# Three PSUM banks for the attention scores, with the rotated transpositions sharing two banks

## The chip, the core and the metric

One core of one Trainium2 chip runs the kernel. The metric is the device time of one launch in microseconds (us), the median of several runs. PE is TensorE's matmul, PEld its weight load, DVE VectorE, ACT ScalarE, POOL GpSimd, SP SyncE. PSUM is where PE writes its results; the kernel hands it out in eight banks, each of 512 float32 values on 128 partitions.

## The reference

The reference is a two-layer encoder trunk over 1024 tokens of width 1024, in float32. Layer 0 mixes tokens with windowed attention, layer 1 with a gated linear recurrence; each also has 4 cross-attention heads into 256 memory tokens, and ends with a convolutional feed-forward layer. The change is in layer 0's mixer:

```python
def mixer_window_attn(u, mem_kv, w_in, sink, w_out, pos):
    q, k, v, xq = jnp.split(u @ w_in, [ATT_Q_W, ATT_Q_W + ATT_KV_W, ATT_Q_W + 2 * ATT_KV_W], axis=-1)
    q = rope(q.reshape(bsz, t, 16, 64), pos)
    k = rope(k.reshape(bsz, t, 4, 64), pos)
    o = window_gqa_sink(q, k, v, sink).reshape(bsz, t, ATT_Q_W)
    return jnp.concatenate([o, memory_cross_attn(xq, mem_kv)], axis=-1) @ w_out
```

In `window_gqa_sink`, 16 query heads share 4 key heads, four to one. The tokens form 8 blocks of 128. A block's queries see the keys of their own block and of the two beside it, less those further than 128 tokens away, and the softmax has one more term per head, the sink.

## The kernel before

All products are made in float32 parts: an operand is split into a high part, rounded by an ACT cast, and the rest, which DVE subtracts; two or three matmuls take the place of one.

The function `window` computes layer 0's mixer. The source says what is to be done and in which buffer; a planner then orders the instructions of each engine with its own estimates of durations. An instruction that stands earlier in the source has the higher priority, and one of lower priority goes in where PE would otherwise have nothing ready. Each engine then runs its queue strictly in that fixed order. A tile has a tag, and a tag has a number of buffers (`bufs`); a new tile of a tag waits until one of them is free, and a buffer is free when the last reader of its tile is done.

The work runs over four groups `g`, each with four query heads and one key head.

- `proj(g)` projects a group. Its `token(t)` is called for the eight token tiles: 24 matmuls into a bank `pj`, then DVE multiplies by cosine and sine, POOL adds the two into the rotated row `rq` (five buffers), and the values go to `v`.
- `turn(b, rqs)` transposes four of these rows, for half `b` of the tokens. It makes three tiles: `w` 0 and 1 are two query heads each, `w` 2 the keys. Each tile takes four transpositions on PE (line 310), one for each row, and is emptied by an ACT cast and a DVE subtraction for the keys (`split`, lines 85 and 86), or by two of each for the queries (lines 318 to 321). These tiles have a bank of their own, tag `ptq`, except for the queries of group 0's first half, which use the two banks `pt`.
- `attend(g)` goes through the eight blocks. A block has four scores (one per head), each two matmuls (lines 362 and 363) into a bank `ps`; DVE adds the mask, takes the row maximum and writes the score to `sm` (line 365), and with that frees the bank. ACT then makes the exponentials (line 372), ACT and DVE divide, and for each of three key blocks PE transposes the four heads' probabilities into a bank `pt` (line 388), which `split` empties; two matmuls (lines 391, 392) add the product with `v` into the bank `po`. `sm` has three buffers.
- `cross_unit` does half of one cross-attention head. Eight of these are spread behind the blocks, and they use the same tags `pj`, `ps`, `pt` (line 232) and `po`.

The source order is `proj(0)`, then `attend(g)` and `proj(g + 1)` for `g` = 0, 1, 2, then `attend(3)`; so in the planned order the projection of the next group lies in the gaps of this group's attention.

The PSUM banks in this stage are two `pj`, one `ptq`, two `ps`, two `pt` and one `po`, eight together.

Under `attend(3)`, where there is nothing left to project, the output projection fills the gaps. `wo0.begin` computes its first partial sums from heads 0 to 11, eight token tiles one after another; `bank()` gives them the banks of its list in turn (`pj`, `pj`, `ptq`). `wo0.finish` adds a second part: the four cross heads (`cross`) and then heads 12 to 15 (`kept`), which `attend(3)` has just made and `split_moved` (line 341) splits. Its first six token tiles use the same list; from the seventh on it has further banks, allocated where the attention's were.

Of the kernel before, what the change touches and what calls it, by code (L numbers as in the profile page):

```python
# [8 lines left out]
F32 = mybir.dt.float32  # L9
# [9 lines left out]
P = 128  # L19
T = 1024  # L20
D = 1024
NT = T // P
# [24 lines left out]
def build(tc, A, out):  # L47
# [20 lines left out]
    def wunit(src, n=1024, pl=None, eng=None, tags=None):  # L68

        tg = tags or (("wh", "wl") if pl is None else ("xwh", "xwl"))  # L70
        h = (pl or ring).tile([P, 1024], F32R, tag=tg[0], name=tg[0])
        l = (pl or ring).tile([P, 1024], F32R, tag=tg[1], name=tg[1])
        raw = stg.tile([P, 1024], F32, tag="st", name="st")[:, :n]
        nc.sync.dma_start(raw, src)
        act.copy(h[:, :n], raw)  # L75
        (eng or dve).tensor_tensor(l[:, :n], raw, h[:, :n].bitcast(F32), op=ALU.subtract)  # L76
        return h, l

    def mm3(o, ah, al, bh, bl, first, last):
        pe.matmul(o, ah, bh, start=first, stop=False)  # L80
        pe.matmul(o, ah, bl, start=False, stop=False)  # L81
        return pe.matmul(o, al, bh, start=False, stop=last)  # L82

    def split(h, l, src):
        act.copy(h, src)  # L85
        dve.tensor_tensor(l, src, h.bitcast(F32), op=ALU.subtract)  # L86
# [155 lines left out]
    def window():  # L242
        ea = tc.alloc_tile_pool(name="attn0", bufs=1, reuse_waits="tile")
        ap_ = tc.alloc_tile_pool(name="attn", bufs=2, side="right", reuse_waits="tile")
        psq = tc.alloc_tile_pool(name="aps0", bufs=1, space=PSUM, reuse_waits="tile")
        psp = tc.alloc_tile_pool(name="aps", bufs=1, space=PSUM, side="right", reuse_waits="tile")
# [5 lines left out]
        nc.sync.dma_start(sk, A["a_sink"].to_broadcast([P, 16]))  # L252
        c4 = lambda ap: ap.rearrange("p (h a c) -> p h a c", a=2, c=32)

        tags = {"pj": ("pj", 2, psq), "ps": ("ps", 2, psp), "pt": ("pt", 2, psp), "po": [lambda: psp.tile([P, 512], F32, tag="po", bufs=1, name="po")] * 2, "sm": 3}
        xhead = [None]
        def pair(kind, i):
            pl, n = (ea, 1) if kind == "x" else (ap_, 2)
# [4 lines left out]
        def proj(g):  # L263
            us = [wunit(A["wqkv"][g, u], 768, eng=pool if u < QKV_POOL[g] else None) for u in range(4)]
            qs = [[None] * 2 for _ in range(4)]
            kvp = ap_ if g % 2 else ea
            kh = kvp.tile([P, T], F32R, tag="kh", bufs=1, name="kh")
            kl = kvp.tile([P, T], F32R, tag="kl", bufs=1, name="kl")
            v = kvp.tile([P, NT, P], F32R, tag="v", bufs=1, name="v")
            def token(t):  # L270
                ps = psq.tile([P, 384], F32, tag="pj", bufs=2, name="pj")
                for k in range(KT):
                    wh, wl = us[k // 2]
                    c = slice((k % 2) * 384, (k % 2 + 1) * 384)
                    m = slice(t * P, (t + 1) * P)
                    mm3(ps, uh[:, k, m], ul[:, k, m], wh[:, c], wl[:, c], k == 0, k == KT - 1)
                if g == 0:
                    with tc.issue_after(roped[0].ins) if t else nullcontext():
                        rooted(t, cos[:, t], sin[:, t].rearrange("p a b -> p (a b)"))
                t1 = ea.tile([P, 320], F32, tag="t1", bufs=1, name="t1")  # L280
                t2 = ea.tile([P, 320], F32, tag="t2", bufs=1, name="t2")
                rq = ea.tile([P, 384], F32, tag="rq", bufs=5, name="rq")
                cb = bc(cos[:, t, :].unsqueeze(1).unsqueeze(1), [P, 5, 2, 32])
                sb = bc(sin[:, t, :, :].unsqueeze(1), [P, 5, 2, 32])
                dve.tensor_tensor(c4(t1), c4(ps[:, :320]), cb, op=ALU.mult)
                roped[0] = dve.tensor_tensor(c4(t2), c4(ps[:, :320])[:, :, ::-1, :], sb, op=ALU.mult)
                pool.tensor_tensor(rq[:, :320], t1, t2, op=ALU.add)
                done = pool.tensor_tensor(rq[:, 320:], t1[:, 256:], t2[:, 256:], op=ALU.add)
                sum_steps[0].send(done)
                cast = act.activation(v[:, t, :64], ps[:, 320:], AF.Copy, scale=rs0[:, t:t + 1])  # L290
                if g == 0 and t + 5 < NT:
                    tag = ("kh", "kl", "v")[t]
                    row = ap_.tile([P, NT, P] if tag == "v" else [P, T], F32R, tag=tag, bufs=1, name="row").bitcast(F32)
                    row = row.rearrange("p a b -> p (a b)") if tag == "v" else row
                    nc.sync.dma_start(row, A["x"][(t + 5) * P:(t + 6) * P, :])
                    with tc.issue_after(cast.ins):
                        act.activation(row, row, AF.Square, accum_out=xss[:, t + 5:t + 6])
                dve.scalar_tensor_tensor(v[:, t, 64:], ps[:, 320:], rs0[:, t:t + 1], v[:, t, :64].bitcast(F32),
                                         op0=ALU.mult, op1=ALU.subtract)
                return rq  # L300

            def turn(b, rqs):
                hs = slice(b * 512, (b + 1) * 512)
                for w in range(3) if (g, b) not in ((0, 0), (3, 1)) else (2, 0, 1):
                    if g or b or w == 2:
                        tp = psq.tile([P, 4, P], F32, tag="ptq", bufs=1, name="ptq")
                    else:
                        tp = psp.tile([P, 4, P], F32, tag="pt", bufs=2, name="ptq")
                    for tt in range(4):
                        pe.transpose(tp[:, tt, :], rqs[tt][:, w * P:(w + 1) * P], ident)  # L310
                    tp = tp.rearrange("p a b -> p (a b)")
                    if w == 2:
                        split(kh[:, hs], kl[:, hs], tp)
                    else:
                        lo, hi = slice(0, 64), slice(64, 128)
                        q0, q1 = [ap_.tile([P, 512], F32R, tag="qs", bufs=8, name="qs") for _ in range(2)]
                        qs[2 * w][b], qs[2 * w + 1][b] = q0, q1
                        act.copy(q0[lo], tp[lo])
                        dve.tensor_tensor(q0[hi], tp[lo], q0[lo].bitcast(F32), op=ALU.subtract)
                        act.copy(q1[hi], tp[hi])  # L320
                        dve.tensor_tensor(q1[lo], tp[hi], q1[hi].bitcast(F32), op=ALU.subtract)

            kept = (qs, kh, kl, v)
            if g == 0:
                rqs = [token(t) for t in range(5)]
                turn(0, rqs[:4])
                attend(0, kept, range(3))
                turn(1, rqs[4:] + [token(t) for t in range(5, NT)])
            else:
                for b in range(2):  # L330
                    turn(b, [token(t) for t in range(4 * b, 4 * b + 4)])
            return kept
# [3 lines left out]
        marks, moved = {}, []  # L336
# [7 lines left out]
        def attend(g, qkv, blocks=range(NT)):  # L344
            qs, kh, kl, v = qkv
            for b in range(2):
                for nn in range(4):
# [7 lines left out]
                    w = (hi - lo) * P  # L355
                    mo = (lo - (n - 1)) * P
                    sm = ap_.tile([P, 4, 384], F32, tag="sm", bufs=3, name="sm")
                    st = {x: ap_.tile([P, 4], F32, tag=x, name=x) for x in ("mx", "nm", "es", "su", "rd")}
                    for j in range(4):
                        s = psp.tile([P, 384], F32, tag="ps", bufs=2, name="ps")  # L360
                        m = slice(nn * P, (nn + 1) * P)
                        pe.matmul(s[:, :w], qs[j][b][:, m], kh[:, lo * P:hi * P], start=True, stop=False)
                        pe.matmul(s[:, :w], qs[j][b][:, m], kl[:, lo * P:hi * P], start=False, stop=True)
                        hd = 4 * g + j
                        dve.tensor_tensor_reduce(out=sm[:, j, :w], in0=s[:, :w], in1=wmask[:, mo:mo + w],
                                                 scale=1.0, scalar=sk8[:, hd:hd + 1], op0=ALU.add, op1=ALU.max,
                                                 accum_out=st["mx"][:, j:j + 1])
# [16 lines left out]
                    po = psp.tile([P, 4, P], F32, tag="po", bufs=1, name="po")  # L384
                    for c in range(hi - lo):
                        tp = psp.tile([P, 4, P], F32, tag="pt", bufs=2, name="pt")
# [32 lines left out]
        for g in range(3):  # L419
            attend(g, cur, range(0 if g else 3, NT))  # L420
            cur = proj(g + 1)
# [2 lines left out]
        attend(3, cur)  # L424
        wo0.open()
        y0 = wo0.w1.tile([P, NT, 512], F32, bufs=1, name="y0")
        wo0.begin(psq, ("pj", "pj", "ptq"), [y0[:, t, :] for t in range(NT)], {6: marks[3, 2], 7: marks[3, 2]})
        psp.release()
        ap_.release()

# [1044 lines left out]
    wo0 = Out(0, A["x"], "wout0", list(range(NT)))  # L1475
    wo1 = Out(1, h2d, "wout1", [4, 5, 6, 7, 0, 1, 2, 3])
    start()
    window()
    wo0.finish()
    x0.release()  # L1480
# [91 lines left out]
```

## Time and profile before

| | |
|---|---|
| Median of 3 runs | 2661.35 us (2661.11 to 2663.44) |
| The profiled execution | 2660.75 us, of which the span in the profile is 2658.9 |
| Granted PE clock | 0.997 of full, mean |
| Busy share of the span | PE 98%, PEld 82%, DVE 67%, ACT 53%, POOL 18% |
| First projection of layer 0 to the last product of its attention | about 55 to 500 us |

A row of the waits says which engine and line waited, after the arrow for which engine and line, then the total in us, how often, and the longest. A row of one tile's instructions has line, engine, operation, tile written and tiles read, count, minimum, median and maximum in ns, and the first and last start in us. A row in order of time has the start, the duration, the instruction, how many stand there merged (x), and in brackets the idle time before it and what ended that. A matmul's duration includes its run through the pipeline, so the distance between two starts is what PE spends on one. Idle time of an engine that is not the bottleneck costs nothing.

### The profile page before, as it was taken

Reading aid. Unit: us, or ns where it says so; the run is one execution under the profiler, and the core shown is the slowest. Engines: PE = TensorE matmul, PEld = TensorE weight load, DVE = VectorE, ACT = ScalarE, POOL = GpSimd, SP = SyncE. Lnnn points to the kernel's source line nnn. Section 1 sums busy time; section 2 is a strip of 40 time slices with the busy share of each in tenths; the row PEclk is TensorE's granted clock in tenths of the full one; section 3 lists DMA queues with packets and bytes.
Section 4 is the critical chain, followed back from the end, with each engine's and each line's share of the span. In section 5 each row is a group of like instructions: output and inputs, shape, how many; then the busy total and the mean of one; then the engine's idle time right before and its main releaser. Section 6 shows DMA issues by size and latency. Waiting matters only on the chain. (4 is left out here: it accounts for less than half of the span.)

```text
span 2658.9 us, 39054 instructions
## 1 busy us (share of the span) xinstructions
PE 2605.2 (98%) x14420; PEld 2185.9 (82%) x14420; DVE 1771.2 (67%) x2948; ACT 1399.1 (53%) x2534; POOL 472.2 (18%) x520
## 2 busy tenths in 40 slices
PE   8999999999999999999999999999999999999998
PEld 7888887788888888887888878888887788888887
DVE  6678886578555565477677675876757755656447
ACT  6467676545444445455464554656534444445453
POOL 0321010211111100032234131231211111110013
PEclk9999999999999999999999999999999999999999
DMA  9782222367777756674236251103336778785666
GB/s 353 243 176 58 74 86 83 101 193 194 198 201 195 206 154 221 215 265 151 84 112 167 66 124 54 53 25 113 127 105 195 194 193 209 198 202 170 205 207 236
DMA packets 195727, 425.92 MB, mean 160 GB/s; under 512 B 20048, under 2 KB 56272, under 8 KB 189904
## 3 DMA queue, kind: packets, MB, share of 16 engines
q1 hardware_dynamic: 161552, 324.06, 37.6%
q0 software_dynamic: 24544, 90.19, 16.3%
q10 hardware_dynamic: 9440, 9.19, 1.0%
q8 instruction: 113, 1.85, 0.3%
q14 instruction: 78, 0.64, 0.1%
HBM read 330.04 MB, written 116.39 MB: 168 GB/s over the span
## 5 line engine op out<-in xcount | busy, mean ns | idle before, releaser
L86 DVE TENSOR_TENSOR wl<-st,wh 128x1024 fp32r<-128x1024 f32 (+1 forms) x238 | 261.4, 1105 | 316.8 <-ACT wh L85 294.1
L85 ACT CAST wh<-st 128x1024 fp32r<-128x1024 f32 (+1 forms) x238 | 222.4, 937 | 288.7 <-PE X L574 186.5
L80 PE MATMUL pj<-uh,wh 128*128 128x512 f32 x512 | 203.6, 398 | 2.2 <-DVE q L1129 0.8
L574 PE MATMUL X<-wl,wh 128*128 128x512 f32 x528 | 205.0, 390 | 0.3 <-DVE wl L86 0.3
L574 PE MATMUL X<-wh,wl 128*128 128x512 f32 x528 | 204.9, 389 | 0.0
L81 PE MATMUL pj<-ul,wh 128*128 128x512 f32 x512 | 202.4, 395 | 0.0
L82 PE MATMUL pj<-uh,wl 128*128 128x512 f32 x512 | 202.3, 395 | 0.0
L574 PE MATMUL X<-wh 128*128 128x512 f32 x528 | 198.6, 390 | 0.0
L80 PE MATMUL pj<-wh,uh 128*128 128x384 f32 (+1 forms) x512 | 189.4, 372 | 5.0 <-DVE gs L1115 2.6
L82 PE MATMUL pj<-wh,ul 128*128 128x384 f32 (+1 forms) x512 | 187.7, 367 | 0.0
L81 PE MATMUL pj<-wl,uh 128*128 128x384 f32 (+1 forms) x512 | 187.2, 366 | 0.0
L76 DVE TENSOR_TENSOR wl<-st,wh 128x1024 fp32r<-128x1024 f32 (+1 forms) x91 | 113.9, 1256 | 30.9 <-ACT wh L75 29.8
L574 PE MATMUL V<-uh,wh 128*128 128x512 f32 x336 | 130.7, 389 | 0.0
L574 PE MATMUL V<-ul,wh 128*128 128x512 f32 x336 | 130.7, 389 | 0.0
L574 PE MATMUL V<-uh,wl 128*128 128x512 f32 x336 | 130.7, 389 | 0.0
L75 ACT CAST wh<-st 128x1024 fp32r<-128x1024 f32 (+1 forms) x97 | 97.8, 1014 | 37.5 <-PE pj L81 16.4
L574 PEld LDWEIGHTS X<-wl,wh 128*128 128x128 f32 x528 | 99.1, 188 | 21.6 <-DVE wl L86 1.2
L574 PEld LDWEIGHTS X<-wh,wl 128*128 128x128 f32 x528 | 99.1, 188 | 20.7
L574 PEld LDWEIGHTS X<-wh 128*128 128x128 f32 x528 | 99.1, 188 | 20.5
L80 PEld LDWEIGHTS pj<-uh,wh 128*128 128x128 f32 x512 | 96.5, 189 | 21.7 <-DVE q L1129 1.2
L82 PEld LDWEIGHTS pj<-uh,wl 128*128 128x128 f32 x512 | 96.5, 189 | 19.0
L81 PEld LDWEIGHTS pj<-ul,wh 128*128 128x128 f32 x512 | 96.5, 188 | 18.6 <-DVE ul L86 0.4
(411 smaller groups left out, 7149.2 us busy)
## 6 DMA issues: line engine op xcount, KB each, us to landing
st<-hid SPq DMA_DIRECT2D x154, 256.0 KB, 3.4
st<-in_ffw_dram SPq DMA_DIRECT2D x108, 256.0 KB, 3.7
w2s<-in_ffw_dram POOLq DMA_DIRECT2D x24, 1024.0 KB, 8.0
st<-in_ffw_dram SPq DMA_DIRECT2D x46, 512.0 KB, 4.3
hid<-tt SPq DMA_DIRECT2D x88, 256.0 KB, 4.7
st<-w2s SPq DMA_DIRECT2D x88, 256.0 KB, 3.2
sx<-in_ffw_dram SPq DMA_DIRECT2D x84, 256.0 KB, 3.9
sy<-in_ffw_dram SPq DMA_DIRECT2D x42, 512.0 KB, 6.4
```

Of the source, the lines that this page charges most:

```text
L75: act.copy(h[:, :n], raw)
L76: (eng or dve).tensor_tensor(l[:, :n], raw, h[:, :n].bitcast(F32), op=ALU.subtract)
L80: pe.matmul(o, ah, bh, start=first, stop=False)
L81: pe.matmul(o, ah, bl, start=False, stop=False)
L82: return pe.matmul(o, al, bh, start=False, stop=last)
L85: act.copy(h, src)
L86: dve.tensor_tensor(l, src, h.bitcast(F32), op=ALU.subtract)
L574: last = pe.matmul(o, x, y, start=new, stop=e, skip_group_check=not first)
```

## The change

The scores get a third bank: the tag `ps` has three buffers. The bank `ptq` goes: all rotated queries' and keys' tiles are allocated with the tag `pt`, whose two banks also serve the probabilities' transpositions of attention and cross-attention. The output projection's first list of banks has two entries instead of three; `finish` then allocates four further banks instead of three.

```diff
-        tags = {"pj": ("pj", 2, psq), "ps": ("ps", 2, psp), "pt": ("pt", 2, psp), ...
+        tags = {"pj": ("pj", 2, psq), "ps": ("ps", 3, psp), "pt": ("pt", 2, psp), ...
...
             def turn(b, rqs):
                 hs = slice(b * 512, (b + 1) * 512)
                 for w in range(3) if (g, b) not in ((0, 0), (3, 1)) else (2, 0, 1):
-                    if g or b or w == 2:
-                        tp = psq.tile([P, 4, P], F32, tag="ptq", bufs=1, name="ptq")
-                    else:
-                        tp = psp.tile([P, 4, P], F32, tag="pt", bufs=2, name="ptq")
+                    tp = psp.tile([P, 4, P], F32, tag="pt", bufs=2, name="ptq")
                     for tt in range(4):
                         pe.transpose(tp[:, tt, :], rqs[tt][:, w * P:(w + 1) * P], ident)
...
-                        s = psp.tile([P, 384], F32, tag="ps", bufs=2, name="ps")
+                        s = psp.tile([P, 384], F32, tag="ps", bufs=3, name="ps")
...
-        wo0.begin(psq, ("pj", "pj", "ptq"), [y0[:, t, :] for t in range(NT)], {6: marks[3, 2], 7: marks[3, 2]})
+        wo0.begin(psq, ("pj", "pj"), [y0[:, t, :] for t in range(NT)], {6: marks[3, 2], 7: marks[3, 2]})
```

More of the change, by code (lines that the diff above doesn't have):

```diff
@@ L253, in window @@
         c4 = lambda ap: ap.rearrange("p (h a c) -> p h a c", a=2, c=32)
-        tags = {"pj": ("pj", 2, psq), "ps": ("ps", 2, psp), "pt": ("pt", 2, psp), "po": [lambda: psp.tile([P, 512], F32, tag="po", bufs=1, name="po")] * 2, "sm": 3}
+        tags = {"pj": ("pj", 2, psq), "ps": ("ps", 3, psp), "pt": ("pt", 2, psp), "po": [lambda: psp.tile([P, 512], F32, tag="po", bufs=1, name="po")] * 2, "sm": 3}
         xhead = [None]
```

## The prediction

> **What bounds the kernel now.** I read the page's head first, then busy time by stretches, then the waits of PE, because PE is nearly always busy and a gain can only come out of its idle time.
>
> ```profile
> span 2658.9 us, 39054 instructions
> PE 2605.2 (98%) x14420; PEld 2185.9 (82%) x14420; DVE 1771.2 (67%) x2948; ACT 1399.1 (53%) x2534; POOL 472.2 (18%) x520
> ```
>
> The span is 2658.9 us; the profiled execution took 2660.75, and the median of the runs is 2661.35, so 1.85 us lie around the span and this execution stands 0.6 below the median. The change works inside the window attention, from the first projection (55 us) to the last probability product (500 us), and in the output projection behind it. The next rows are us of stretch, then busy time and number of instructions of each engine, the granted clock and the DMA share.
>
> ```profile
> core 0: us, PE busy (x) PEld busy (x) DVE busy (x) ACT busy (x) POOL busy (x), PEclk, DMA share, GB/s
> 55.00:110.00 55.00, 53.32 (x299) 50.08 (x298) 36.11 (x108) 28.52 (x62) 23.05 (x35) 1.00 0.88 301
> 110.00:200.00 90.00, 83.07 (x472) 73.92 (x471) 67.26 (x179) 55.52 (x146) 22.91 (x30) 0.98 0.72 160
> 200.00:300.00 100.00, 96.81 (x563) 86.86 (x562) 84.10 (x224) 70.12 (x177) 14.70 (x20) 1.00 0.28 71
> 300.00:400.00 100.00, 92.54 (x533) 81.00 (x532) 80.97 (x212) 72.46 (x180) 11.27 (x16) 1.00 0.26 79
> 400.00:500.00 100.00, 95.10 (x463) 76.61 (x462) 65.84 (x166) 64.33 (x150) 0.00 (x0) 1.00 0.23 68
> 500.00:560.00 60.00, 60.00 (x277) 49.33 (x277) 38.23 (x61) 26.78 (x58) 20.12 (x19) 1.00 0.56 181
> ```
>
> The five rows to 500 us add to 420.84 busy of 445: PE is idle for 24 us in the whole stage, and then for none. DVE is the next engine, at 84 and 81 of 100 in the middle. PE's own waits between 55 and 500 us (engine and line that waited, what it waited for, total, times, longest):
>
> ```profile
> PE ps L362 <- DVE mx L365: 8.9, 14, 1.5
> PE po L392 <- DVE pl L86: 3.3, 5, 1.2
> PE ps L362 <- ACT kh L85: 0.6, 1, 0.6
> PE ptq L310 <- DVE qs L321: 0.3, 1, 0.3
> ```
>
> The largest is a score product that waits for its bank: the reduction of the score two before (line 365) has not read it yet. The single bank of the rotated transpositions (ptq) costs PE 0.3 us. First, longest and last of those fourteen:
>
> ```profile
> 136.28 0.44 PE L362 MATMUL ps<-kh,qs 128*128 128x384 f32 x1 [0.79 <-DVE mx L365]
> 335.62 0.44 PE L362 MATMUL ps<-kh,qs 128*128 128x384 f32 x1 [1.54 <-DVE mx L365]
> 474.69 0.39 PE L362 MATMUL ps<-kh,qs 128*128 128x256 f32 x1 [1.04 <-DVE mx L365]
> ```
>
> **The change, part by part.** No arithmetic and no transfer is added, removed or put on another queue; banks change hands, and with them the order in which the planner lays out PE's queue. The durations that price it (minimum, median, maximum in ns, then first and last start in us):
>
> ```profile
> L392 PE MATMUL po<-pl,v x88: 387/397/504, 110.3 to 499.1; 128*128 128x512 f32 x88
> L365 DVE CUSTOM_DVE_ANT_0 sm<-ps,wmask,sk x128: 455/610/621, 85.9 to 476.5; 128x384 f32<-128x384 f32 x96, 128x256 f32<-128x256 f32 x32
> L85 ACT CAST ph<-pt x104: 560/587/607, 105.4 to 496.9; 128x512 fp32r<-128x512 f32 x104
> L86 DVE TENSOR_TENSOR pl<-pt,ph x104: 659/683/693, 106.2 to 497.6; 128x512 fp32r<-128x512 f32 x104
> L318 ACT CAST qs<-ptq x16: 568/580/585, 79.9 to 414.7; 64x512 fp32r<-64x512 f32 x16
> L319 DVE TENSOR_TENSOR qs<-ptq,qs x16: 683/685/685, 80.5 to 415.9; 64x512 fp32r<-64x512 f32 x16
> L320 ACT CAST qs<-ptq x16: 581/583/585, 81.3 to 421.2; 64x512 fp32r<-64x512 f32 x16
> L321 DVE TENSOR_TENSOR qs<-ptq,qs x16: 692/693/694, 82.2 to 422.2; 64x512 fp32r<-64x512 f32 x16
> ```
>
> *The third score bank.* Each wait ends one reduction earlier, 0.61 us. Six of the fourteen are longer than that and lose 0.61 each (3.7 us); the other eight, 2.9 us together, go. That is 6.6 us saved; the ends are nothing (DVE, busy 84 of 100, stays behind and PE meets it at the next product) and the whole 8.9. I take 6.6, as the waits are short beside one reduction. What is late next is the po product behind line 86. The Trainium skill's page Perfetto Trace Analysis, section Optimization Strategy, reads a gap that repeats on the engine that should be saturated as a sign of too few buffers for the next tile. The fourteen waits agree, and by that rule alone all 8.9 us go and the time is 2651.9.
>
> *The rotated transpositions lose their bank.* A ptq tile takes four transpositions, one for each token tile, and the code may put in the first as soon as that token is projected; the bank stays taken until the fourth token comes. The trace shows that this is done, and that it takes as many banks as there are: in group 0's first half, where two pt banks and ptq were all open to it, each token was transposed into three tiles at once (x3 below). Later, with ptq alone, one tile stayed open from 212.41 to 241.21.
>
> ```profile
> 69.40 0.49 PE L310 MATMUL ptq<-ident,rq 128*128 128x128 f32 x3
> 212.41 0.27 PE L310 MATMUL ptq<-ident,rq 128*128 128x128 f32 x1
> 241.21 0.27 PE L310 MATMUL ptq<-ident,rq 128*128 128x128 f32 x1
> ```
>
> After the change these tiles can take one or both of the two banks that the probabilities' transpositions need. Groups 1 to 3 have two such holds each. The rows below are these six stretches, from first to fourth transposition, with only the instructions that touch the pt tiles; the PE number in brackets counts the probabilities' transpositions that stood there.
>
> ```profile
> 129.00:145.00 16.00, 1.20 (x8) 1.00 (x8) 0.00 (x0) 0.55 (x2) 1.00 0.93 182
> 169.20:191.00 21.80, 2.83 (x22) 2.36 (x20) 3.31 (x5) 3.01 (x6) 1.00 0.74 155
> 212.40:241.30 28.90, 5.41 (x36) 4.37 (x36) 6.71 (x10) 4.45 (x8) 1.00 0.40 84
> 272.70:279.00 6.30, 0.60 (x4) 0.50 (x4) 0.00 (x0) 1.17 (x2) 1.00 0.57 156
> 336.10:372.50 36.40, 5.76 (x40) 4.79 (x41) 6.78 (x11) 5.04 (x9) 1.00 0.21 63
> 393.90:402.60 8.70, 0.22 (x3) 0.00 (x0) 1.36 (x2) 0.59 (x1) 1.00 0.80 241
> sum 118.10, PE 111.50 PEld 99.71 DVE 92.85 ACT 76.59 POOL 31.05; mean PE 18.58 PEld 16.62 DVE 15.47 ACT 12.77 POOL 5.18
> ```
>
> They hold 118.1 us and 113 transpositions, 28 tiles. The last row is the sum for all instructions: PE was busy 111.5 of the 118.1, since the very tokens that the open tile waits for are work for PE. So while a tile is open PE need not starve. What is exposed is the end of the hold: attention has three probability tiles (sm) ready and no bank, the last token has been projected, and PE waits while one query tile is emptied: 0.580 + 0.685 + 0.583 + 0.693 = 2.54 us. Six holds make 15.2 us. The lower end is a gain of 0.9 us: three tiles pass through two banks instead of one, and the waits for kh (0.6) and line 321 (0.3) go; I count that gain in any case. The upper end is that each of the 28 tiles pays for a single bank: about 0.60 us of four transpositions (estimated from the 0.49 us for three above) + 0.587 + 0.683 = 1.87, which is 52 us. I take 15.2, much nearer the lower end, because of the 111.5. Group 0's second half also holds a bank, but before the first probabilities; I charge nothing. A PE instruction that waits has all of PE's queue behind it, scores and projections too; ACT's cast, DVE's subtraction and then the product po wait for it. On POOL the rotated sums may find their rq tile later, with the weight-sum DMAs behind them; POOL is busy 11 to 23 us of each of those stretches, so I charge nothing, and the cost without that cover would be tokens that come later. The same page, section Matmuls, wants independent products rotated through different banks so that emptying one overlaps the next; of the pt tiles the change takes that away, and by that rule the sum leans to its upper end.
>
> *The output projection has two banks instead of three under the last attention.* Its first partial sums fill PE's gaps there. A sum of the second round begins with the cross heads (12 products) and then stays open until attention delivers heads 12 to 15 for that tile. The rows are the products pb alone, then two of them in time, then PE's next wait.
>
> ```profile
> 461.50:471.80 10.30, 8.37 (x34) 6.24 (x34) 0.00 (x0) 0.00 (x0) 1.00 0.18 53
> 471.80:479.90 8.10, 0.03 (x1) 0.00 (x0) 0.00 (x0) 0.00 (x0) 1.00 0.26 65
> 470.98 0.39 PE L80 MATMUL pb<-xwh,oh 128*128 128x512 f32 x1
> 471.21 0.39 PE L81 MATMUL pb<-xwl,oh 128*128 128x512 f32 x1
> 479.98 0.50 PE L80 MATMUL pb<-xwh,uh 128*128 128x512 f32 x1 [0.60 <-ACT uh L341]
> ```
>
> The 34 products are the cross parts of three tiles; then all three banks are open and nothing fills PE for 8 us, until line 341 brings the heads. With two banks the third tile's 12 products at 0.23 us each can't be started: 2.8 us of cover less. Between nothing (they fill later gaps) and 2.8 I take 2.8, as PE already waits there. From 500 us on the other bank's products cover each emptying, and I charge nothing; if that cover failed, the row of 60.00 busy would show it.
>
> *Sum*: 2660.75 − 6.6 − 0.9 + 15.2 + 2.8 = 2671.25, said as 2671 us, 0.4% slower.
>
> **The rivals.**
>
> *Faster, by the score bank.* The place is the fourteen waits, the price 6.6 + 0.9 us, and it decides if the holds cost less than 2 us in all (with the two-bank term hidden as well). For it speaks that PE was kept busy 111.5 of 118.1 us in the holds, and that the planner lays attention before projections wherever both are ready. Against it speaks x3 at 69.40. It gives 2653.
>
> *The same.* Only the two long holds, 28.9 and 36.4 us, cost their 2.54 each, as the others see few tiles (8 and 22, 4 and 3 transpositions). Then 2660.75 − 7.5 + 5.1 + 2.8 = 2661. It is also where the time ends if the planner's new order simply shifts waits about.
>
> *Much slower.* Both banks taken for all of each hold, and the 28 tiles each paid for: 2660.75 − 7.5 + 52 + 2.8 = 2708. Against it speak DVE and ACT, which have scores and exponentials to do for three blocks meanwhile.
>
> **How the numbers follow.** A measurement of this kernel can tell about 0.2% (5.3 us) from no change. My forecast, slower by more than that with 2671 as its value and 2666 to 2685 as its own range, has 0.48; much slower 0.09; the same 0.25; faster 0.18. That is slower 0.57, same 0.25, faster 0.18. The range of 2654 to 2692 takes in the same-case and the upper part of the faster one, and leaves out about half of the faster and most of the much slower one, under 2 in 10.
>
> **What would show it.** In the profile after, the wait of line 362 on line 365 should fall from 8.9 us to 2 or 3. Line 310 should show x2 or more at single tokens inside groups 1 to 3, and lines 388 and 232 should stand still between those tokens. New waits of PE (lines 310, 388, 391 or 392) on lines 86, 319 or 321 should add to about 15 us. The busy time of PE from 55 to 500 us stays at 421 us while the last line-392 product moves from 499 to about 509. Between 461 and 480 us the products pb should be 12 fewer. I am wrong if the holds do not open two tiles, or if they do and PE's idle time stays at 24 us.

## The result and the profile after

The changed kernel takes 2691.94 us (median of 4 runs, 2690.47 to 2693.07) against 2661.68 (2661.11 to 2663.44) in the same comparison: ratio 1.0112, 95% interval 1.01 to 1.0125. It is 30 us slower; the prediction said 10 us slower, 2654 to 2692. The sign was right and the size three times too small: 2691.94 lies just inside the end of the range, and outside the forecast's own range, 2666 to 2685. The profiled execution took 2692.77 us, its span is 2691.0.

From here on the changed kernel's lines in the attention stand three lower than before: 310 is 307, 318 and 321 are 315 and 318, 362 and 365 are 359 and 362, 388 is 385, 391, 392 and 395 are 388, 389 and 392.

The head of the page after, then its busy time by the same stretches as before (busy time and instructions of each engine, granted clock, DMA share).

```profile
span 2691.0 us, 39060 instructions
PE 2618.2 (97%) x14420; PEld 2198.7 (82%) x14420; DVE 1769.4 (66%) x2948; ACT 1403.2 (52%) x2534; POOL 467.1 (17%) x520
...
55.00:110.00 55.00, 54.02 (x303) 50.88 (x302) 34.59 (x112) 29.39 (x67) 22.59 (x35) 1.00 0.87 304
110.00:200.00 90.00, 79.14 (x430) 69.30 (x429) 63.83 (x162) 55.63 (x135) 20.88 (x27) 0.91 0.61 142
200.00:300.00 100.00, 91.21 (x512) 80.08 (x512) 74.08 (x204) 66.01 (x166) 16.13 (x22) 0.96 0.37 86
300.00:400.00 100.00, 91.93 (x500) 81.58 (x500) 73.60 (x212) 65.79 (x174) 8.31 (x12) 0.95 0.15 44
400.00:500.00 100.00, 92.12 (x465) 77.86 (x464) 68.15 (x165) 64.63 (x141) 3.42 (x6) 0.97 0.31 91
```

The span grew by 32.1 us, and two things make it up. PE is idle for 72.8 us instead of 53.7 (span less busy time), which is 19.1. And the same 14420 instructions keep PE busy for 2618.2 us instead of 2605.2, which is 13.0: they run slower, and the clock column, 0.98 to 1.00 before, reads 0.91 to 0.97 from 110 us on.

The place is mostly the attention. First and last start of the last probability product, after:

```profile
L389 PE MATMUL po<-pl,v x88: 387/397/796, 109.1 to 523.4; 128*128 128x512 f32 x88
```

Attention ends 24.3 us later (523.4 against 499.1). From there to the feed-forward layer's first product it is 5.9 us longer (81.8 against 75.9); that stretch is the output projection, taken up at e_begin2 below. The 1.9 us that are left lie in the feed-forward layers and behind, and I give them no cause. PE's waits from 55 to 500 us after the change:

```profile
PE ptq L307 <- DVE qs L318: 9.8, 3, 4.0
...
PE ps L359 <- ACT kh L85: 3.8, 4, 1.5
...
PE ps L359 <- DVE mx L362: 2.7, 4, 0.9
```

The score wait has gone from 8.9 us to 2.7, as the prediction's first step had it. At the top stand three waits of a rotated tile for the emptying of the one two before it. All three lie where one group's attention ends and the next begins. The first of these changes, in order of time, PE's rotated transpositions, cross-attention transpositions and scores only:

```profile
188.87 0.60 PE L232 MATMUL pt<-ident,xp 128*128 128x128 f32 x4
190.50 0.60 PE L307 MATMUL ptq<-ident,rq 128*128 128x128 f32 x4
191.65 0.60 PE L307 MATMUL ptq<-ident,rq 128*128 128x128 f32 x4
194.28 1.08 PE L307 MATMUL ptq<-ident,rq 128*128 128x128 f32 x4 [2.04 <-DVE qs L318]
196.91 1.01 PE L359 MATMUL ps<-kh,qs 128*128 128x256 f32 x3 [1.53 <-ACT kh L85]
```

The row at 188.87 is the last transposition of group 0, cross units included. Only then come group 1's rotated tiles, each with all four transpositions at once, only two of them at a time, the keys' as the third; and only then group 1's first score. Before the change the rotated tiles of group 1 had started at 129.0 in their own bank, and group 1's first score came before the last probability transposition of group 0:

```profile
184.20 0.28 PE L362 MATMUL ps<-kh,qs 128*128 128x256 f32 x1
...
189.98 0.60 PE L388 MATMUL pt<-ident,sm 128*128 128x128 f32 x4
```

So groups 0 and 1, which had overlapped, now follow one another, and so do 1 and 2; groups 2 and 3 had not overlapped before either. I call this place the change of groups below.

### The profile page after: what moved, and what is told of

Read it like the earlier page. It is cut to its first block, busy times and chain, and to the rows that moved or that the text cites. A ratio compares the mean times of both kernels' runs of the same rounds, so it can differ in the third digit from the quotient of the medians.

```text
span 2691.0 us, 39060 instructions
## 1 busy us (share of the span) xinstructions
PE 2618.2 (97%) x14420; PEld 2198.7 (82%) x14420; DVE 1769.4 (66%) x2948; ACT 1403.2 (52%) x2534; POOL 467.1 (17%) x520
## 5 line engine op out<-in xcount | busy, mean ns | idle before, releaser
L571 PEld LDWEIGHTS X<-wh 128*128 128x128 f32 x528 | 99.2, 188 | 20.8 <-issue 0.5
```

Of the source, the lines that this page charges most:

```text
L571: last = pe.matmul(o, x, y, start=new, stop=e, skip_group_check=not first)
```

## The experiments

The theory with which I went in was: banks of one tag are handed out in the order of the source, so a shared tag puts the next group's rotated tiles behind everything of this group, however many banks there are. The rival: two banks are too few for two kinds of tile.

**One group shares (a_share_g1).** Kernel before, no bank taken away:

```diff
-                    if g or b or w == 2:
+                    if g != 1 and (g or b or w == 2):
                         tp = psq.tile([P, 4, P], F32, tag="ptq", bufs=1, name="ptq")
```

> The kernel before, with one edit: the six rotated tiles of group 1 take the tag pt; the bank ptq stays for the other groups, the scores keep two banks, the output projection its three. Theory (banks of one tag are handed out in the order of the source): group 1's six tiles stand in the source behind all of group 0's probabilities and cross units, so one of the three serial handovers seen after the change appears, between group 0 and group 1, and only there. The change's kernel is about 25 us late at the end of attention after three handovers, so 2670 us (2667 to 2674); line 310 shows x4 for group 1, after the last line-232 transposition of group 0. Rival (too few banks for two kinds of tile): no bank is missing here, two pt and one ptq are there as before, so 2661, at most 2 us off. Rival of the prediction (tiles opened token by token hold the banks): two holds of 2.54 us, 2667, with x1 to x3 of line 310 between tokens of group 1.

2675.43 us (ratio 1.0049, 1.0037 to 1.0062), 13.8 slower. The trace shows at the change from group 0 to group 1, and only there, the same picture as the changed kernel:

```profile
189.22 0.60 PE L232 MATMUL pt<-ident,xp 128*128 128x128 f32 x4
190.87 0.60 PE L310 MATMUL ptq<-ident,rq 128*128 128x128 f32 x4
...
194.89 0.63 PE L310 MATMUL ptq<-ident,rq 128*128 128x128 f32 x4 [2.29 <-DVE qs L321]
197.35 0.50 PE L362 MATMUL ps<-kh,qs 128*128 128x256 f32 x2 [1.83 <-ACT kh L85]
```

The loss is there, at the one place where the tag is shared. It doesn't tell the theory from the rival: at this change the bank ptq lies unused, so the two kinds of tile have two banks between them, just as in the changed kernel.

**Three shared banks (b_shared3) and two (d_after_ps2).** Both are the changed kernel with two score banks; b gives the third bank to the shared tag, d leaves it empty.

```diff
-"ps": ("ps", 3, psp), "pt": ("pt", 2, psp)
+"ps": ("ps", 2, psp), "pt": ("pt", 3, psp)     # b_shared3; the tiles' bufs alike
+"ps": ("ps", 2, psp), "pt": ("pt", 2, psp)     # d_after_ps2
```

> The changed kernel, with the third bank moved from the scores to the shared tag: pt has three banks for both kinds of tile, ps two. Theory (order of the source): a third bank doesn't change who is in front of whom; the rotated tiles of group g+1 still come after the last probabilities and cross units of group g, three handovers remain, and the scores have lost their third bank: 2690 us (2682 to 2700). Rival (too few banks): these are the same three banks for the same tiles as before the change, now handed out freely, so 2661 to 2665.

> The changed kernel with two score banks; the eighth bank stays empty in attention. It gives the worth of the third score bank where everything else is as after the change. If the waits of the scores on line 362 (the reduction) are worth what the trace shows (8.9 us before, 2.7 after): 2698 us. If the handovers between groups set the time and the score waits lie inside them, nothing: 2692.

b took 2669.71 us (1.0034, 1.0022 to 1.0046), d 2693.15 (1.012, 1.0106 to 1.0134). b fits neither account. It has the same source order, and its groups follow one another just as in the changed kernel, with the first rotated tile behind the last cross-unit transposition and the first score behind that:

```profile
188.77 0.66 PE L232 MATMUL pt<-ident,xp 128*128 128x128 f32 x4 [0.71 <-DVE pl L86]
189.46 0.63 PE L307 MATMUL ptq<-ident,rq 128*128 128x128 f32 x4
...
195.06 0.48 PE L359 MATMUL ps<-kh,qs 128*128 128x256 f32 x2
```

From the start of a group's last probability transposition to the next group's first score it is 15.0, 18.4 and 21.9 us in b at the three changes, and 14.7, 15.2 and 20.2 in the changed kernel; before, it is −5.8, −4.6 and 8.9, negative where the groups overlap. Yet b has only 8 us of the loss, where my theory had said 2690, and its attention ends at 502.1 us, 3.0 later than before; d's ends at 522.6. So the order alone is not what costs 30: the third shared bank takes 20.5 us off the end of attention with the order as it is. And d is as slow as the changed kernel: the third score bank is worth 1.2 us, which the intervals can't tell from nothing. The wait for the score reduction is 3.5 us in d, so most of its fall from 8.9 to 2.7 comes without that bank. To see where b wins against d, here are 45 us of each around the three changes of groups, beginning 8 to 10 us before the first line-232 transposition at the end of the group: the kernel before (with 55 to 607 us as a fourth row), b, d, the changed kernel, and a_share_g1.

```profile
182.00:227.00 45.00, 44.10 (x250) 39.19 (x248) 34.40 (x94) 30.26 (x78) 9.95 (x11) 1.00 0.62 147
273.00:318.00 45.00, 42.68 (x223) 34.02 (x222) 36.24 (x93) 31.50 (x79) 4.90 (x4) 1.00 0.26 78
376.00:421.00 45.00, 40.97 (x216) 33.73 (x215) 36.73 (x86) 29.93 (x65) 5.50 (x6) 1.00 0.41 122
55.00:607.00 552.00, 527.84 (x2823) 456.70 (x2822) 409.72 (x994) 341.85 (x806) 101.12 (x132) 1.00 0.46 130
```

```profile
176.00:221.00 45.00, 40.48 (x225) 34.17 (x224) 36.23 (x86) 30.33 (x68) 11.77 (x14) 1.00 0.60 144
268.00:313.00 45.00, 41.98 (x224) 35.59 (x223) 31.80 (x75) 27.77 (x63) 7.33 (x8) 1.00 0.28 82
381.00:426.00 45.00, 41.25 (x227) 35.89 (x227) 35.20 (x75) 29.82 (x64) 4.58 (x8) 1.00 0.49 147
```

```profile
178.00:223.00 45.00, 36.91 (x189) 30.22 (x188) 31.36 (x71) 25.86 (x55) 10.59 (x11) 0.92 0.58 144
279.00:324.00 45.00, 38.42 (x193) 31.70 (x192) 27.61 (x60) 24.26 (x51) 7.64 (x8) 0.92 0.24 76
401.00:446.00 45.00, 37.89 (x188) 30.88 (x188) 31.58 (x68) 28.37 (x58) 3.42 (x6) 0.92 0.44 130
```

```profile
175.00:220.00 45.00, 37.64 (x180) 31.38 (x179) 30.05 (x75) 25.50 (x61) 8.92 (x11) 0.85 0.60 144
274.00:319.00 45.00, 38.89 (x190) 32.41 (x190) 27.87 (x64) 24.16 (x53) 7.65 (x8) 0.89 0.25 72
396.00:441.00 45.00, 38.77 (x204) 33.63 (x203) 28.67 (x65) 24.49 (x51) 4.57 (x8) 0.92 0.42 123
```

```profile
174.00:219.00 45.00, 36.82 (x178) 30.62 (x177) 29.19 (x63) 23.45 (x50) 10.23 (x11) 0.89 0.57 144
280.00:325.00 45.00, 43.72 (x243) 37.54 (x241) 34.51 (x95) 32.82 (x80) 6.90 (x6) 1.00 0.27 81
389.00:434.00 45.00, 40.99 (x217) 33.83 (x216) 36.22 (x83) 29.98 (x66) 5.48 (x6) 1.00 0.41 122
```

The number in the first brackets is how many matmuls PE got done. The sums of three are 689 before, 676 with three shared banks, 570 and 574 with two. A matmul of this stage takes 0.187 us of PE on average (527.84 / 2823). So the 115 matmuls that the changed kernel misses at its three changes are 21.5 us, and the 106 between b and d are 19.8 of the 23.4 us between their times. In a_share_g1 the shared change misses 72 (178 against 250), 13.5 us, of 13.8 measured; its other two miss none. Most of the loss is therefore at the changes of groups, and takes two things together: a tag that both kinds of tile share, and only two banks in it.

**Two banks, not shared (c_own_ptq).** Three score banks, one bank ptq, one bank pt:

```diff
-"ps": ("ps", 2, psp), "pt": ("pt", 2, psp)
+"ps": ("ps", 3, psp), "pt": ("pt", 1, psp)     # the tiles' bufs alike
```

> Three score banks as in the change, but the two other banks are not shared: one is ptq for the rotated tiles, one is pt for all probabilities. The output projection has its three banks. Theory (order of the source): the same number of banks as after the change for the same tiles, but two orders that do not wait for each other, so no handover: PE's gaps between groups go, the score waits stay near 2 us, and a single bank for 104 probability tiles costs something, up to some 10 us: 2655 to 2672. Rival (too few banks): two banks in all for the two kinds, and the probabilities are worse off than after the change, so 2690 us or more.

2787.11 us (1.0474, 1.046 to 1.0488). My theory fell by more than 100 us: the probabilities can't do with one bank at all. Its probability products wait for the cast of their own tile, and 7.5 us more for its subtraction, 55 to 607 us:

```profile
PE po L391 <- ACT ph L85: 30.7, 28, 3.5
```

**The output projection's list alone (e_begin2).** Kernel before, but `bank()` uses two of the three banks until the further ones exist:

```diff
-            pl, tag, n = self.banks[self.used % len(self.banks)]
+            pl, tag, n = self.banks[self.used % (2 if self.l == 0 and len(self.banks) == 3 else len(self.banks))]
```

> The kernel before, with one edit: until the further banks of the output projection exist, its partial sums take turns on two banks (pj, pj) in place of three. Everything in attention is as before. The third term of the prediction's sum, alone: 2664.5 us (2.8 us of cover lost between 461 and 480 us). If later gaps take the same products, nothing: 2661 to 2662.

2658.81 us (0.9993, 0.9984 to 1.0002): no loss, and 2.8 us (1.0011) is outside the interval. The products pb from 461.5 to 479.9 us:

```profile
461.50:479.90 18.40, 13.36 (x51) 8.78 (x49) 1.10 (x2) 0.00 (x0) 1.00 0.20 58
```

They are not 12 fewer than the 34 of before but 17 more. But this is not the whole of the change's edit. Behind the two banks e_begin2 goes on with ptq and three further banks, the changed kernel with four further ones. Here are the products pb from the end of attention to the feed-forward layer's first product, after the change and before it:

```profile
523.40:605.20 81.80, 76.17 (x324) 60.50 (x324) 7.07 (x11) 5.46 (x16) 1.00 0.54 170
```

```profile
499.10:575.00 75.90, 71.84 (x306) 57.12 (x306) 6.54 (x10) 5.33 (x16) 1.00 0.55 179
```

After the change 252 of these products are done when attention ends, before it 270, so 18 more are left. b and d have the same 324 and 81.8 us as the change, e_begin2 306 and 75.8. h_turn_pj below has the change's list and yet 302 and 76.2 us, so the list alone does not decide it. Which part of the edit does was not tried.

So, each measured against the kernel before in its own comparison: sharing three banks, with the change's list for the output projection, +8.1; taking one of the three away +23.4; giving it to the scores −1.3; together, but for rounding, the 30.3 of the change. Of the 8.1, 3.0 are there at the end of attention; the output projection's stretch is 5.9 longer.

**Another place for the rotated tiles (h_turn_pj).** The changed kernel, with the tiles in the projections' two banks:

```diff
-                    tp = psp.tile([P, 4, P], F32, tag="pt", bufs=2, name="ptq")
+                    tp = psq.tile([P, 4, P], F32, tag="pj", bufs=2, name="ptq")
```

> The changed kernel with one edit: the rotated tiles take the projections' two banks (pj) in place of the probabilities' two (pt). As many banks as after the change, three for the scores; the rotated tiles now stand, in the source, between the two halves of their own group's tokens and no longer behind the probabilities of the group before. Theory (the order of the source puts them behind): the handovers go, the projections pay up to 2.5 us for each of the eight halves where PE has no attention to do; 2655 to 2672. Rival (what costs is the missing bank, wherever it is missing): 2680 us or more, as in the two kernels with two shared banks.

2709.42 us (1.018, 1.0166 to 1.0194), worse than the change: the rival's number. A part is lost in group 0 already, where the projections' banks are the tiles' too: from 100 to 110 us PE is busy for 5.62 of the ten. How the rest divides was not followed.

**Another source order, with the change's banks (f6_400) and with those of before (g6_400).** The next group's first half is projected and turned after block 5, the second half before the cross units, with a higher priority for what it was put in front of:

```diff
-            attend(g, cur, range(0 if g else 3, NT))
-            cur = proj(g + 1)
+            attend(g, cur, range(0 if g else 3, 6))
+            nxt, half = proj(g + 1)
+            half(0)
+            with tc.high_priority(400):
+                attend(g, cur, range(6, NT))
+            half(1)
+            with tc.high_priority(400):
+                cross(g, 1)
+            cur = nxt
```

> The changed kernel (three score banks, rotated tiles and probabilities share two banks) with the source in another order: the next group's first half is projected and turned between blocks 5 and 6 of this group's attention, its second half between block 7 and the cross units; blocks 6 and 7 and the cross units keep a priority ahead of the projection. No bank is added. Theory (order of the source): the rotated tiles are no longer behind all of the group's probabilities, so next scores can start while the last ones are worked off; PE's three waits of 2 to 4 us on line 318 go and a good part of the 30 us comes back: 2665 to 2682. Rival (two banks are too few for both): no better than after the change, 2688 us or more, with the probabilities now waiting in the middle of the group.

> The source order of the kernel f6_400 (next group's halves turned between blocks 5 and 6 and before the cross units) on the banks of the kernel before: a bank of its own for the rotated tiles, two for the probabilities, two for the scores. f6_400 was 44 us slower than before although its source order lets the next group in earlier. If sharing two banks is what costs there too, this one is near the kernel before, 2657 to 2672, and f6_400 is 33 us or more behind it. If the new source order itself costs (projections drawn forward, attention pushed back), this one is slow by itself, 2680 us or more.

f6 took 2705.56 us (1.0166, 1.0152 to 1.018): getting the tiles in earlier cured nothing. g6 took 2656.18 (0.9979, 0.9971 to 0.9988), so the order itself does no harm, and the change's banks cost 49 us in it, 43.4 of them by the end of attention (537.8 against 494.4). Around the changes of groups, f6 first, then g6:

```profile
160.00:210.00 50.00, 41.60 (x207) 34.47 (x207) 33.31 (x76) 27.01 (x65) 8.52 (x12) 0.86 0.58 139
260.00:310.00 50.00, 38.91 (x184) 31.15 (x185) 30.71 (x79) 29.37 (x72) 3.51 (x7) 0.86 0.16 43
```

```profile
160.00:210.00 50.00, 48.58 (x287) 43.32 (x286) 39.51 (x114) 35.09 (x94) 5.19 (x8) 0.95 0.56 136
260.00:310.00 50.00, 48.62 (x284) 43.30 (x283) 37.06 (x109) 33.22 (x90) 2.31 (x4) 0.95 0.18 52
```

The same two stretches hold 391 matmuls with the shared pair and 571 without. My repair by order failed: moving the place at which the two kinds meet in two banks moved the loss, and did not lessen it.

**Keys first.** The third tile at a change of groups is the keys', without which no score starts. Put first, in the changed kernel (j_keys_first), with three shared banks (k1_b_keys) and in e_begin2 (k2_e_keys):

```diff
-                for w in range(3) if (g, b) not in ((0, 0), (3, 1)) else (2, 0, 1):
+                for w in (2, 0, 1):
```

> The changed kernel with the keys' tile first in every half (w in the order 2, 0, 1). No bank and no place in the source is changed. With two banks at a handover the third tile waits until the first is emptied, and the keys stand third now; without them no score can start. If that wait (2.0, 3.8 and 4.0 us at the three handovers, and 3.8 us of scores that wait for kh) makes the handovers dear, putting the keys first saves 2 to 4 us at each: 2680 to 2687. If it is that everything stands behind the last probabilities, PE runs dry anyway until exponentials of the next group are made: 2690 to 2693.

> b_shared3 (three banks shared by both kinds of tile, two score banks) with the keys' tile first in every half. With two shared banks keys first was worth about 5 us. If it is the third tile's wait for a bank that keys first shortens, there is none with three banks: 2668 to 2671. If the keys are simply needed first, 2664 to 2667.

> e_begin2 (banks of before, two banks in the output projection's first list) with the keys' tile first in every half. The rotated tiles have a single bank of their own, so the order of the three decides when the next group's scores can start; but they start long before the last probabilities of the group are done, and PE's waits for kh are 0.6 us in all: 2657 to 2660, no difference to e_begin2 that can be told. If the scores' start is what bounds the change of groups, 2654 or less.

j took 2687.1 us (1.0082 to 1.0109, which overlaps the change's interval), k1 2678.11 (1.0061, 1.0048 to 1.0075), 8 us slower than b where neither account allowed it, k2 2659.07 (0.9986, 0.9978 to 0.9995). This decides nothing about the wait for the keys. It does show that a small new order in the source can move the time by 8 us, so differences of that size between kernels planned anew have no cause yet by being measured; b's +8.1 is no more.

**The two edits that did no harm, together (m_g6_begin2).**

> The two edits that were no slower than before, together: the source order of g6_400 (0.2% faster than before) and the two-bank list of e_begin2 for the output projection. If their gains add (6.3 and 2.4 us), 2653 us; if both only fill the same gaps under the last attention, 2656 as g6_400 alone.

2657.82 us (0.9986, 0.9977 to 0.9995): the gains don't add. The lowest median is g6_400's, 6 us or 0.2% under the kernel before, though its interval overlaps those of m, k2 and e; it leaves the banks as they were.

## Why the prediction was right in sign and wrong in size

*The third score bank, −6.6 us.* The wait fell to 2.7 us, as forecast, but hardly by the third bank: d, with two score banks, waits 3.5 us on that reduction, not 8.9. That PE comes there late with other things would explain it; this was not followed. The bank's measured worth is 1.2 us. The step that failed here is the one that took a sum of waits for time. The Trainium skill, Perfetto Trace Analysis, section Optimization Strategy, says that such a gap can mean too few buffers; the price of all 8.9 us that the prediction drew from it did not hold.

*The rotated tiles, +15.2 us.* This is the step that weighs most, and it failed in its mechanism first. I took tiles opened by their first token and held over four; in groups 1 to 3 the tiles at the changes of groups get their four transpositions at once, since the two banks are not given to them until the group before is through. So the six holds did not happen. The emptying of one query tile, 2.54 us in my sum, is indeed waited for, but at three places: 2.04, 3.83 and 3.96, the 9.8 us at the top of the waits. The rows I had from group 0, with nothing in front of it in the source, could not show this; what I should have read is the order of the calls, `attend(g)` and then `proj(g + 1)`, together with the shared tag and its two banks. Its size, by the end of attention, was 23.5 us in d, without the third score bank (522.6 against 499.1): 3.0 with three shared banks, as in b, and 20.5 for the missing one. The prediction had 15.2 less the 0.9 that it counted as a gain. Since the holds did not happen, that the sign came out right is in part luck.

*What was charged at nothing.* I named POOL's rotated sums, and that the cost without their cover would be tokens that come later. The cover went. POOL's waits for a transposition between 55 and 560 us, before and after:

```profile
POOL rq L287 <- PE pt L388: 31.4, 5, 8.6
...
POOL rq L287 <- PE ptq L310: 26.0, 2, 15.4
```

```profile
POOL rq L287 <- PE ptq L307: 66.5, 5, 25.0
POOL rq L287 <- PE pt L385: 53.1, 2, 46.3
```

They are 57.4 us before and 119.6 after. There are five rotated rows; when they are full the projections, which are PE's filler, stand still, just when attention has nothing else to offer. That would explain why PE runs dry there rather than for one emptying only. The same two waits add to 56.5 us in b and 110.1 in d, which fits, but to 49.7 in a_share_g1, which lost 13.8 us all the same. So this stays a guess; a kernel with more rows was not tried.

*PE's busy time.* I said that it stays at 421 us from 55 to 500. It is 408.4, with 36.6 idle in place of 24.2, and the work that is left over runs later. That PE's instructions could become slower was not in the sum at all: 13 of the 32 us of span are added busy time.

*The output projection, +2.8 us.* Too small. By e_begin2 alone the lower end, nothing, would be right, but that kernel has only a part of the edit. In the changed kernel 18 products, not 12, were put off behind the attention, and the stretch there grew by 5.9 us. With the 24.3 of the attention that is 30.2 of the 32.1 us of span.

*The banks' number.* By the Trainium skill, Perfetto Trace Analysis, section Matmuls, which wants independent products rotated through different banks, the sum was to lean to its upper end, and the runs went that way: 23.4 us from three banks to two, and 126 over the kernel before in c_own_ptq, with a single bank.

## What to carry to other kernels

Before two kinds of tile share a set of buffers, read in which order the source asks for them: where buffers are handed out in that order, what overlapped through two sets can become serial. Then ask how many buffers the set has where the two kinds meet: with three the serial order cost 3 us of attention, with two 23. Price that place, here three changes of groups in 400 us, and ask what fills the bound engine there. A wait that repeats is a bound on what removing it can bring, not the gain: 6 us of score waits vanished, 5 of them without the third bank too, and the bank brought 1 us. And an experiment that is to price one part of an edit has to hold the whole of that part: e_begin2 did not.

## What the runs showed of the hardware

A gap on PE can cost more than itself. After the change PE is busy 0.34 of the two us from 178 and 0.78 of the next two, and then this (the same columns as above):

```profile
178.00:180.00 2.00, 0.34 (x4) 0.10 (x2) 1.21 (x5) 2.00 (x7) 0.00 (x0) 1.00 0.93 310
180.00:182.00 2.00, 0.78 (x2) 0.47 (x3) 2.00 (x4) 0.35 (x1) 0.00 (x0) 0.65 0.71 260
182.00:184.00 2.00, 2.00 (x10) 1.74 (x10) 0.92 (x3) 1.17 (x2) 0.00 (x0) 0.50 0.61 197
184.00:186.00 2.00, 2.00 (x7) 1.51 (x7) 1.32 (x2) 0.66 (x2) 0.00 (x0) 0.50 0.04 10
186.00:188.00 2.00, 2.00 (x11) 1.82 (x10) 1.28 (x2) 1.10 (x2) 0.00 (x0) 0.65 0.00 0
188.00:190.00 2.00, 1.76 (x10) 1.27 (x9) 0.78 (x2) 1.52 (x3) 0.00 (x0) 1.00 0.61 131
```

The granted clock is at half for some 7 us, if the two rows of 0.65 are partly at full and partly at half, and the longest probability product takes 0.796 us where the median is 0.397. The Trainium skill, page TensorE: Matmul & The Clock Gate, section Part 1: The HAM clock gate, describes it: half clock after an idle window of about 3.4 us, full clock again after about as long a busy one. The rows above agree as to the half clock, although PE was not wholly idle in the gap; the full clock came back later, some 5 us after PE was busy without a break (182 to about 187).

Over whole kernels, each against the profile before, the changed kernel has 19.1 us more idle time of PE and 13.0 more busy time for the same 14420 instructions, at a granted clock of 0.990 in place of 0.997. The same two numbers are 20.8 and 9.7 in d (clock 0.994), 68.7 and 57.1 in c_own_ptq (0.980), and 7.5 and 1.2 in b (0.998). So each us of idle time came with 0.2 to 0.8 us more busy time, and least of it in b, where the clock stayed up. Not all of it need be slower work: a matmul's duration includes its run through the pipeline, which shows as busy time before each gap, and in c_own_ptq the weight loads grew by only 28.2 us (2214.1 against 2185.9).

The clock column alone is no proof of lost time: g6_400's profile reads 0.945 over the whole execution, at 2658.54 us, while its other executions read 0.995 to 0.997 at 2653.27 to 2657.34; its feed-forward products take 0.389 us as before.
